# The second q quad of a sliding-window attention made whole and rotated ahead of the attention's rounds

## The chip, the cores and the metric

The kernel runs on one core of one Trainium2 chip. The metric is the device time in microseconds (us); the median of three runs before the change is 1546.49 us (1546.46 to 1546.75). Engines are named as in the profile: PE (matrix products), PEld (its weight loads), DVE and ACT (elementwise work), POOL, and SP, which issues nearly all transfers. Each engine runs its own instructions strictly in the order in which the built program lists them, and waits on semaphores where one needs another engine's result.

## The reference

One layer of a decoder on 1024 tokens of width 1024, all in float32, shortened to what matters here:

```
h = rms_norm(x, ln1_g)
rq, rk, rv, rg, aq, ak, av, gate_a, gate_b = split(h @ w_in + b_in)
branch_a = (silu(rg) * group_norm(retention(rotary(rq), rotary(rk), rv))) @ w_ret_out
aq = rotary(aq.reshape(B, S, 16, 64), pos);  ak = rotary(ak.reshape(B, S, 2, 64), pos)
ay = sliding_window_sink_attention(aq, ak, av, sinks)      # window 128, blocks of 128, softmax with a sink
branch_b = ay @ w_attn_out
x = x + (sigmoid(gate_a) * branch_a + sigmoid(gate_b) * branch_b) @ w_out
x = x + (silu(rms_norm(x) @ w_ffn_gate) * (rms_norm(x) @ w_ffn_up)) @ w_ffn_down
return rms_norm(x, lnf_g)
```

The change lies in the part that makes the attention's q, rotates it, and runs the attention.

## The kernel before, in words

Precision: a float32 operand is split into a high part (a rounding copy on ACT, names with h) and a low part (a subtraction on DVE, names with l). A product is then three PE products per 128-row slice of the contraction: high by high, high by low, low by high (lines 178, 179, 180). One such triple is called a *step*; eight steps fill one 128x512 result bank.

The 16 q heads are made in four *quads* of four heads. A quad (`QuadQ`, `quad_q`) has two halves of the sequence (512 tokens each) and two column groups z (first and second half of each head's elements), so four banks `aq<quad><z><half>` and 32 steps. When a bank is full ACT evicts it with the bias (line 493, `q<quad><z><half>`). When both z of a half are there, `rotation` (lines 508 to 544) makes the rotary of that half: six elementwise products and sums on DVE (line 517, tiles q, st1, st2), two rounding copies on ACT (line 533), two subtractions on DVE (line 536), four stores to a scratch tensor in DRAM and four reads back in the layout the attention needs (lines 524, 529). These pieces are put into a list, `tasks`. For quad 0 the list is emptied at once by `all_tasks`; for the later quads each round of the attention takes one entry.

Beside the quads the list `items` holds eight `Gate`s of 16 steps each (banks `acc_g`). The order is quad 0, quad 1, gate 8, quad 2, gate 9, quad 3, then the other gates. Before an item's products its weights are loaded, rounded (`wh_aq` line 452, `wh_g` line 473, on ACT) and their low part is taken (lines 453, 474, on DVE); this preparation of the next item stands at the 24th step of a quad (or the first or fifth of a gate). The raw weights have two buffers.

The attention runs in 34 *rounds*. Round i works on block i of 32 (quad by quad, eight blocks of 128 tokens each): PE transposes the probabilities of block i-2 (line 619, `pT`), makes the scores of block i (line 584, `s`, one bank pair), DVE and ACT mask them and take the minimum (lines 593 to 596; for the first block of a quad four fused mask-and-minimum instructions at line 599), ACT takes the exponentials of block i-1 (line 607), DVE normalises (610, 611). Then a number of *fill steps* of the items follow on PE, and at the round's end the products with v for block i-2 (line 638, `pv`). Probabilities are split too: rounding copy on ACT (621), low part (622) and masked difference (627) on DVE.

How many fill steps stand in each round is set by three numbers: `early` steps are spread over the first `turn` rounds, `late` over the rest; what is then left of the items runs at the end. Within the rounds a context `in_order` pins PE, SP, ACT, DVE and POOL to the order in which the code emits. What is emitted ahead of it is placed by a list scheduler, which can set it between instructions of the rounds on each engine. In both kernels 28 of the items' 224 steps are left after the rounds.

Of the kernel before, what the change touches and what calls it, by code (L numbers as in the profile page):

```python
# [40 lines left out]
def hybrid_block(ctx: ExitStack, tc: tile.TileContext, x, ln1_g, w_in, b_in, ret_norm_g, w_ret_out,  # L41
# [74 lines left out]
    @contextmanager  # L116
    def in_order(*engines):

        traced = nc.cur_bb.bb.instructions
        last = traced[-1]  # L120
        yield
        start = next(k for k in reversed(range(len(traced))) if traced[k] is last) + 1
        prev = {}
        for i in traced[start:]:
            if i.engine in engines:
                if i.engine in prev:
                    tc.add_manual_dep(i, prev[i.engine],
                                      mybir.DependencyInfo(mybir.DependencyClass.NoSync, mybir.DependencyReason.DATA),
                                      reason="in_order")
                prev[i.engine] = i.name  # L130
# [194 lines left out]
    with tc.tile_pool(name="gt", bufs=1, side="right") as gt, tc.tile_pool(name="w1", bufs=1) as w1:  # L325
# [222 lines left out]
        def task():  # L548
            return tasks.pop(0) if tasks else ([], [], [])

        def do(steps):
            for f in steps:
                f()

        def all_tasks():
            while tasks:
                for part in task():
                    do(part)
            while reads:
                reads.pop(0)()  # L560
# [109 lines left out]
        def filling(n):  # L670
            it = items[n]
            while len(it.w) < it.size:
                prep(it)
            at = 23 if it.size == 2 else 4 if n + 1 < len(items) and items[n + 1].size == 2 else 0
            for k, _ in enumerate(it.products()):
                if k == at and n + 1 < len(items):
                    prep(items[n + 1])
                yield
# [5 lines left out]
        open_s("s_wide")  # L684
        fl = Fill([filling(n) for n in range(1, len(items))])
        NU = 4 * NB
        fl.step(20)
        early, late, turn = 118, 58, 21
        with in_order(nc.tensor.engine, nc.sync.engine, nc.scalar.engine, nc.vector.engine, nc.gpsimd.engine):
            u_sink(0)  # L690
            for i in range(NU + 2):
# [449 lines left out]
    def bb_g(n):  # L1141
        def evac(half, pt):
            c = slice(half * 512, half * 512 + 512)
            t = rt.tile([P, 512], F32, tag="r", bufs=2, name=f"tbr{n}{half}")
            nc.sync.dma_start(t, tb_d[8 + n, :, c])
            m = w2.tile([P, 512], F32, tag="mbw", bufs=1, name=f"mb{n}{half}")
            nc.vector.scalar_tensor_tensor(out=m, in0=t, scalar=1.0, in1=pt, op0=ALU.add, op1=ALU.mult)
            nc.sync.dma_start(mb_d[n, :, c], m)
        return dense_g(w_attn_out, n * P, AY, evac, f"bb{n}")
# [160 lines left out]
    fl = Fill([bb_g(n) for n in range(8)])  # L1310
# [51 lines left out]
    with tc.tile_pool(name="w3", bufs=1) as w3:  # L1362
# [52 lines left out]
        late = in_order(nc.vector.engine, nc.scalar.engine)  # L1415
# [448 lines left out]
    early, kept = [], []  # L1864
# [268 lines left out]
```

## Time and profile before

| | |
|---|---|
| median of three runs | 1546.49 us (1546.46 to 1546.75) |
| the profiled execution's own time | 1546.24 us |
| its span, first to last instruction | 1544.1 us |
| PE busy | 1532.1 us (99%) |
| DVE busy | 1024.5 us (66%) |
| ACT busy | 693.5 us (45%) |
| POOL busy | 386.3 us (25%) |
| mean granted PE clock | 0.999 |
| first scores of the attention (round 0) | start at 78.27 us |
| scores of round 31 | start at 259.28 us |

The span is what the instructions cover; the profiled execution's time is 2.1 us more, which lies outside the instructions. The profile page gives shares over the whole span, so the stretch of the attention (78 to some 265 us) has to be read by windows and by the order in time. A PE product is issued before the one ahead has drained, so its busy time covers small waits: the distance from one start to the next tells more than the idle time.

### The profile page before, as it was taken

How to read it: one execution, taken by the hardware profiler on the slowest of the kernel's cores; microseconds unless marked ns; L12 is line 12 of the kernel's file. 1: busy time of each engine (PE TensorE's matmuls, PEld its weight loads, DVE VectorE, ACT ScalarE, POOL GpSimd, SP SyncE). 2: the span in 40 equal slices, each digit the busy share in tenths (PEclk: the TensorE clock that was granted, in tenths of full speed). 3: DMA queues.
4: the chain of work that ended last, by engine and by line, in shares of the span. 5: the costliest groups of instructions: out<-in, count | busy, mean ns of one | idle time of the engine just before them, and what ended most of it. 6: DMA issues, size and time to landing. Idle time of an engine off the chain costs nothing.

```text
span 1544.1 us, 20386 instructions
## 1 busy us (share of the span) xinstructions
PE 1532.1 (99%) x7299; PEld 1279.8 (83%) x7299; DVE 1024.5 (66%) x1590; ACT 693.5 (45%) x1368; POOL 386.3 (25%) x344
## 2 busy tenths in 40 slices
PE   9999999999999999999999999999999999999998
PEld 8888878888888888888888888888888888888886
DVE  7588897884677764887558688444444444688666
ACT  6366666332344454544223465333333333344445
POOL 2011111002233320000120216555555555100001
PEclk9999999999999999999999999999999999999999
DMA  6656474315766647653657103333333333963332
GB/s 229 187 163 189 144 250 166 103 55 175 207 195 196 213 163 262 206 192 117 204 178 253 68 1 123 109 103 103 102 103 103 103 104 108 318 226 96 92 111 118
DMA packets 158001, 236.85 MB, mean 153 GB/s; under 512 B 10603, under 2 KB 81069, under 8 KB 157645
## 3 DMA queue, kind: packets, MB, share of 16 engines
q1 hardware_dynamic: 155292, 227.04, 45.7%
q0 software_dynamic: 2560, 8.39, 1.5%
q8 instruction: 57, 0.93, 0.3%
q14 instruction: 44, 0.35, 0.1%
q10 hardware_dynamic: 48, 0.13, 0.0%
HBM read 156.62 MB, written 74.19 MB: 149 GB/s over the span
## 4 chain that ended last, share of the span: by engine, by line
PE 94%; DVE 3%; DMA 1%; issue 1%; ACT 1%; SPq 0%; POOL 0%; POOLq 0%; DVEq 0%
PE fA L1757 16%; PE wA L1022 8%; PE fB L1757 8%; PE dA L2059 7%; PE dxP L2059 6%; PE wB L1022 4%; PE fC L1757 4%; PE va L865 3%; PE wo L1591 3%; PE woP L1591 2%; PE wC L1022 2%; PE vP L865 2%; PE aq L178 2%; PE aq L179 2%; PE aq L180 2%; PE acc_ba L180 2%
## 5 line engine op out<-in xcount | busy, mean ns | idle before, releaser
L2059 PE MATMUL dA<-dwP,daP 128*128 128x512 f32 x528 | 120.6, 389 | 0.0
L2059 PEld LDWEIGHTS dA<-dwP,daP 128*128 128x128 f32 x528 | 99.0, 188 | 20.7 <-DVE dwP L154 0.2
L2059 PE MATMUL dxP<-dwP,daP 128*128 128x512 f32 x396 | 90.2, 389 | 0.0
L2059 PEld LDWEIGHTS dxP<-dwP,daP 128*128 128x128 f32 x396 | 74.3, 188 | 15.4
L1832 POOL TENSOR_TENSOR xf<-xf 128x512 f32<-128x512 f32 x40 | 63.9, 1598 | 31.0 <-issue 28.8
L734 POOL TENSOR_TENSOR wr_wp<-wr_wp 128x512 f32<-128x512 f32 x12 | 18.2, 1514 | 193.5 <-DVE w0P L154 92.5
L642 POOL DMA_DIRECT2D xy_d<-xy x32 | 23.1, 723 | 157.2 <-ACT xy L641 98.9
L1763 POOL TENSOR_TENSOR xf<-xf 128x512 f32<-128x512 f32 x33 | 47.3, 1435 | 58.9 <-ACT xf L1765 26.9
L1964 POOL TENSOR_TENSOR rs_f<-tot,mhalf 128x1 f32<-128x1 f32 x8 | 4.9, 607 | 205.4 <-DVE tot L1961 205.4
L154 DVE TENSOR_TENSOR dwP<-wd,dwP 128x512 fp32r<-128x512 f32 x77 | 52.8, 685 | 4.8 <-ACT dwP L151 4.8
L607 ACT ACTIVATE sc<-sc,nm 128x129 f32<-128x129 f32 x128 | 50.1, 402 | 3.6 <-DVE nm L599 3.3
L151 ACT CAST dwP<-wd 128x512 fp32r<-128x512 f32 x77 | 47.4, 616 | 9.1 <-PE dA L2059 6.9
L178 PE MATMUL acc_bb<-ay,wh_bb 128*128 128x512 f32 x128 | 51.0, 400 | 0.0
L151 ACT CAST daP<-daP 128x512 fp32r<-128x512 f32 x42 | 26.0, 621 | 54.8 <-PE dxP L2059 26.7
L180 PE MATMUL acc_bb<-ay,wl_bb 128*128 128x512 f32 x128 | 50.3, 393 | 0.0
L178 PE MATMUL acc_g<-h,wh_g 128*128 128x512 f32 x128 | 50.3, 393 | 0.0
L179 PE MATMUL acc_bb<-ay,wh_bb 128*128 128x512 f32 x128 | 50.2, 392 | 0.0
L178 PE MATMUL aq<-h,wh_aq 128*128 128x512 f32 x128 | 50.2, 392 | 0.0
L179 PE MATMUL aq<-h,wh_aq 128*128 128x512 f32 x128 | 50.0, 391 | 0.0
L179 PE MATMUL acc_g<-h,wh_g 128*128 128x512 f32 x128 | 50.0, 391 | 0.0
L734 POOL TENSOR_TENSOR wr_f<-wr_f 128x512 f32<-128x512 f32 x20 | 30.7, 1533 | 77.2 <-DVE t_6P L154 8.6
L178 PE MATMUL acc_ba<-yg,wh_ba 128*128 128x512 f32 x128 | 49.9, 390 | 0.0
(866 smaller groups left out, 4314.5 us busy)
## 6 DMA issues: line engine op xcount, KB each, us to landing
act_d<-xf SPq DMA_DIRECT2D x77, 256.0 KB, 2.1
daP<-act_d SPq DMA_DIRECT2D x21, 512.0 KB, 3.9
q<-q_d SPq DMA_DIRECT2D x32, 256.0 KB, 4.0
xy_d<-xy POOLq DMA_DIRECT2D x32, 256.0 KB, 3.8
wr_daP<-act_d SPq DMA_DIRECT2D x14, 512.0 KB, 6.7
wr_wp<-in_w_in SPq DMA_DIRECT2D x12, 512.0 KB, 5.4
wp<-in_w_in SPq DMA_DIRECT2D x12, 512.0 KB, 5.2
wd<-in_w_ffn_down SPq DMA_DIRECT2D x6, 1024.0 KB
```

The costliest lines, as they stand in the source:

```text
L151: nc.scalar.copy(hi, raw)
L154: return nc.vector.tensor_tensor(out=lo, in0=raw, in1=f32(hi), op=ALU.subtract)
L178: nc.tensor.matmul(pt, hi[:, k, :], xh, start=(k == 0), stop=False)
L179: nc.tensor.matmul(pt, hi[:, k, :], xl, start=False, stop=False)
L180: nc.tensor.matmul(pt, lo[:, k, :], xh, start=False, stop=(k == 7))
L607: nc.scalar.activation(sc[:, j, 0:P + 1], sc[:, j, 0:P + 1], AF.Exp, scale=-1.0, bias=nm[:, j:j + 1], accum_out=den[:, j:j + 1])
L865: nc.tensor.matmul(vbanks[pr][tt], x_[:, c], w[:, u, :], start=(fresh and k + z == 0), stop=(k == 3 and z == 2), skip_group_check=not fresh)
L1022: nc.tensor.matmul(pt, o[:, w, k, :], v, start=(first and k + z == 0), stop=(k == 3 and z == 2), skip_group_check=not first)
L1591: nc.tensor.matmul(bank, v[:, q + u, k, c], w[y][:, k % 2, :], start=(first and z == 0), stop=(last and z == 2), skip_group_check=not tracked)
L1757: nc.tensor.matmul(pt, o[:, w, k, :], v, start=(first and n == 0), stop=(n == 11), skip_group_check=not first)
L1832: nc.gpsimd.tensor_tensor(out=o, in0=a, in1=b, op=op)
L2059: nc.tensor.matmul(banks[tt], a[:, u, c], w[:, v, :], start=(fresh and f + z == 0), stop=(f == NP - 1 and z == 2), skip_group_check=not fresh)
```

## The change

The number of fill steps ahead of the rounds grows from 20 to 32, which is all of quad 1. Then `all_tasks()` is called, so that both halves of quad 1's rotation are emitted ahead of the rounds instead of as entries of the first rounds. The three numbers become 120 steps over the first 24 rounds (five in each) and 44 over the last ten; they were 118 over 21 and 58 over 13. The sum is the same: 20 + 118 + 58 = 32 + 120 + 44 = 196 steps.

```diff
         open_s("s_wide")
         fl = Fill([filling(n) for n in range(1, len(items))])
         NU = 4 * NB
-        fl.step(20)
-        early, late, turn = 118, 58, 21
+        fl.step(32)
+        all_tasks()
+        early, late, turn = 120, 44, 24
         with in_order(nc.tensor.engine, nc.sync.engine, nc.scalar.engine, nc.vector.engine, nc.gpsimd.engine):
             u_sink(0)
```

What it moves, first on ACT at round 0. Names: `sc00` is the score tile of quad 0, block 0, and the line 607 rows are its four exponentials; `q101` and `q111` are evictions of quad 1's second half; the two line 533 rows with `q100` and `st110` are the rounding copies of the rotation of quad 1's first half; `wh_g8` is the rounding copy of the weights of gate 8, the item after quad 1. Before:

```order
L493 ACTIVATE q110_896<-aq110_871,bcol_91 128x512
L607 ACTIVATE sc00_911,den00_913<-sc00_911,nm00_912 128x129 x4
L493 ACTIVATE q101_951<-aq101_898,bcol_91 128x512
L473 CAST wh_g8_953<-wr_g8_840 128x1024
L593 COPY sc01_935<-s01_968 128x4x128
L621 CAST p00_1010<-pT00_1005 128x512
```

And in the changed kernel:

```order
L493 ACTIVATE q110_896<-aq110_871,bcol_91 128x512
L607 ACTIVATE sc00_998,den00_1000<-sc00_998,nm00_999 128x129
L493 ACTIVATE q101_923<-aq101_898,bcol_91 128x512
L607 ACTIVATE sc00_998,den00_1000<-sc00_998,nm00_999 128x129
L533 ACTIVATE q100_869<-st210_957 128x512
L533 ACTIVATE st110_956<-q110_896 128x512
L607 ACTIVATE sc00_998,den00_1000<-sc00_998,nm00_999 128x129 x2
L473 CAST wh_g8_925<-wr_g8_840 128x1024
L452 CAST wh_aq20_1042<-wr_aq20_842 128x512
```

In both the copy of gate 8's weights stands behind the four exponentials of block 0; in the changed kernel the two rounding copies of quad 1's rotation stand between those exponentials.

On DVE at the same place (line 599: mask and minimum of block 0; line 517: rotation of quad 1's first half; `wl_g8`: low part of gate 8's weights) the order in the changed kernel is:

```order
L536 TENSOR_TENSOR q011_808<-q011_808,st101_810 128x512
L517 TENSOR_TENSOR st210_957<-q100_869,atab_186 128x512
L599 ISA sc00_998,nm00_999<-s00_1002,amask_188,nsink_90 128x128
L599 ISA nm00_999 128x1
L517 TENSOR_TENSOR st110_956<-q110_896,atab_186 128x512
L517 TENSOR_TENSOR q100_869<-q100_869,atab_186 128x512
L517 TENSOR_TENSOR st210_957<-st210_957,st110_956 128x512
L517 TENSOR_TENSOR q110_896<-q110_896,atab_186 128x512
L599 ISA sc00_998,nm00_999<-s00_1002,amask_188,nsink_90 128x128
L599 ISA nm00_999 128x1
L517 TENSOR_TENSOR q110_896<-q110_896,q100_869 128x512
L599 ISA sc00_998,nm00_999<-s00_1002,amask_188,nsink_90 128x128
```

Before, the four line 599 instructions stood together behind the first of these rows, and the rotation of quad 1 came only after `wl_g8`. Now the first line 599 instruction stands ahead of five of the six rotation instructions of quad 1's first half, which are spread among the four.

On PE, the products that follow the first scores before:

```order
L180 MATMUL aq101_898<-h0_118,wl_aq10_778 128x512
L584 MATMUL s00_915<-kst_190,q0_675 128x128 x8
L178 MATMUL aq101_898<-h1_119,wh_aq10_777 128x512
L179 MATMUL aq101_898<-h1_119,wh_aq10_777 128x512
L180 MATMUL aq101_898<-h1_119,wl_aq10_778 128x512
```

and in the changed kernel:

```order
L180 MATMUL aq111_931<-h1_119,wl_aq11_835 128x512
L584 MATMUL s00_1002<-kst_190,q0_675 128x128 x8
L178 MATMUL acc_g8_0_1026<-h0_118,wh_g8_925 128x512
L179 MATMUL acc_g8_0_1026<-h0_118,wh_g8_925 128x512
L180 MATMUL acc_g8_0_1026<-h0_118,wl_g8_926 128x512
```

Before, twelve steps of quad 1 still followed the first scores; now the scores stand behind the whole of quad 1, and the first fill product is gate 8's.

## The prediction

> **What bounds the kernel now.** I read the page first, then the attention's stretch by windows, then the order in time around each place where the change moves something.
>
> ```profile
> PE 1532.1 (99%) x7299; PEld 1279.8 (83%) x7299; DVE 1024.5 (66%) x1590; ACT 693.5 (45%) x1368; POOL 386.3 (25%) x344
> PE 94%; DVE 3%; DMA 1%; issue 1%; ACT 1%; SPq 0%; POOL 0%; POOLq 0%; DVEq 0%
> 200.00:220.00 20.00, 19.50 (x102) 15.93 (x100) 18.74 (x29) 13.87 (x40) 2.81 (x6) 1.00 0.89 284
> 220.00:240.00 20.00, 19.35 (x105) 15.97 (x106) 16.63 (x34) 13.74 (x45) 3.83 (x8) 1.00 0.81 278
> ```
>
> PE is busy 99% of the span and makes 94% of the chain of waits. The change neither adds nor removes a PE product, so it can only alter how long PE waits, and a wait that it adds is never made up later: behind the attention there is no slack on PE. In the windows (PE is the second number) only 200 to 240 us shows PE idle, 0.50 + 0.65 = 1.15 us. That is all there is to gain in idle time; in start distances it is somewhat more:
>
> ```profile
> 212.75 0.62 PE L638 MATMUL pv<-p,vev 128*128 128x512 f32 x2
> 213.21 0.63 PE L638 MATMUL pv<-q,vdf 128*128 128x512 f32 x2
> 213.84 0.63 PE L619 MATMUL pT<-ident,sc 128*128 128x128 f32 x4
> 218.88 0.61 PE L638 MATMUL pv<-p,vev 128*128 128x512 f32 x2
> 220.11 0.73 PE L638 MATMUL pv<-q,vdf 128*128 128x512 f32 x2 [0.62 <-DVE q L627]
> 221.02 0.63 PE L619 MATMUL pT<-ident,sc 128*128 128x128 f32 x4 [0.17 <-DVE sc L611]
> 227.32 1.22 PE L584 MATMUL s<-kst,q 128*128 128x256 f32 x8 [0.37 <-DVE nm L599]
> ```
>
> An undisturbed pair of pv products takes 0.46 us (212.75 to 213.21). At 218.88 the next pair starts 1.23 us later, 0.77 too late; it then takes 0.91 to the transposes, 0.45 too long; the scores at 227.32 lose about 0.5. With the small ones (0.17 at 213.84) some **2.0 us** are lost in rounds 22 to 25, all waiting for a DVE that is full with quad 3's rotation.
>
> **Part 1, twelve steps moved ahead of round 0.**
>
> ```profile
> 78.27 1.00 PE L584 MATMUL s<-kst,q 128*128 128x128 f32 x8
> 79.11 0.45 PE L178 MATMUL aq<-h,wh_aq 128*128 128x512 f32 x1
> 79.87 0.40 PE L178 MATMUL aq<-h,wh_aq 128*128 128x512 f32 x1
> 80.56 0.40 PE L178 MATMUL aq<-h,wh_aq 128*128 128x512 f32 x1
> ```
>
> A step takes 80.56 - 79.87 = 0.69 us, 0.23 a product. Twelve push the first scores back by 8.2 us, to about 86.5, and are missing in the rounds: no cost in the sum.
>
> **Part 2, what follows the first scores.** Before, twelve steps of quad 1 (8.2 us), whose weights were ready, covered the time in which block 0 went through DVE and ACT and gate 8's weights were rounded behind it. Now the first product behind the scores needs those weights at once, so this cover is gone. The chain, each instruction behind the one ahead in its engine's order as listed above:
>
> ```profile
> 79.31 0.35 DVE L599 CUSTOM_DVE_ANT_0 sc<-s,amask,nsink 128x128 f32<-128x128 f32 x1 [6.26 <-PE s L584]
> 79.59 0.35 DVE L599 CUSTOM_DVE_ANT_0 sc<-s,amask,nsink 128x128 f32<-128x128 f32 x1
> 67.70 0.69 DVE L517 TENSOR_TENSOR q<-q,atab 128x512 f32<-128x512 f32 x1
> 68.31 0.69 DVE L517 TENSOR_TENSOR st<-q,atab 128x512 f32<-128x512 f32 x1
> 91.05 0.63 ACT L533 ACTIVATE q<-st 128x512 fp32r<-128x512 f32 x1
> 91.58 0.62 ACT L533 ACTIVATE st<-q 128x512 fp32r<-128x512 f32 x1
> 80.17 0.39 ACT L607 ACTIVATE sc<-sc,nm 128x129 f32<-128x129 f32 x1
> 80.55 0.39 ACT L607 ACTIVATE sc<-sc,nm 128x129 f32<-128x129 f32 x1
> 83.30 1.05 ACT L473 CAST wh_g<-wr_g 128x1024 fp32r<-128x1024 f32 x1 [0.47 <-DMA wr_g<-in_w_in]
> 84.39 1.23 DVE L474 TENSOR_TENSOR wl_g<-wr_g,wh_g 128x1024 fp32r<-128x1024 f32 x1 [2.03 <-ACT wh_g L473]
> ```
>
> Counted from the scores' start: DVE's first mask instruction at 1.04 (79.31 - 78.27), taking 0.28; four rotation instructions at about 0.62 (67.70 to 68.31, a little more where one needs the one before) end at 3.8; the second mask instruction 0.28; the fifth rotation instruction, 0.69 to its end, 4.8. Then ACT's two rounding copies, 0.53 apart, until 5.9: the first writes the tile that this fifth instruction reads, so it can't go earlier. Two exponentials at 0.38: 6.65. The copy of gate 8's weights, 1.05: **7.7**. PE could have gone on at 0.84 (79.11 - 78.27), so it stands **6.9 us**. The raw weights are no bound: in the row at 83.30 they had just landed, ahead of this copy's new start at 86.5 + 6.65 = 93.1. Then the third product of the step needs the low part, 1.23 behind the copy, while two products take 0.46: **0.8 us** more.
>
> Queued behind on DVE: the rest of the rotation; on ACT: the eviction of quad 1's last bank and quad 2's weights; on SP the stores of quad 1, wanted only in round 8. PE alone pays. Bounds: the scheduled order fixes the chain, only the rotation instructions' spacing (0.61 to 0.72) and a semaphore's delay move it, 7.0 to 8.5 for both.
>
> **Part 3, the clock after such a wait.** Two places of the trace show what an idle PE costs afterwards.
>
> ```profile
> 1.02 4.02 PE L290 MATMUL warm<-wk 128*128 128x128 bf16 x36 [1.02 <-DVE wk L261]
> 6.82 0.61 PE L290 MATMUL warm<-wk 128*128 128x128 bf16 x8
> 1533.61 3.33 PE L2059 MATMUL dA<-dwP,daP 128*128 128x512 f32 x14
> 1540.00:1541.00 1.00, 0.00 (x0) 0.00 (x0) 0.00 (x0) 0.17 (x1) 0.00 (x0) 1.00 0.00 0
> 1541.00:1542.00 1.00, 0.00 (x0) 0.00 (x0) 0.00 (x0) 0.00 (x0) 0.00 (x0) 0.54 1.02 422
> ```
>
> At the end PE's last product ends at 1536.94; the granted clock is full until 1541.0 and averages 0.54 in the next us, so it halves about 4.1 us after PE falls idle. At the start 36 products take 4.02 us, some 0.11 each, while the later eight take 0.61 with the last one's drain, some 0.06 each: after an idle stretch the first 4.0 us, at most 5.8 (to 6.82), run at about half speed. An idle of 6.9 us is longer than 4.1, so I expect the clock to halve and cost half of 4.0, 2.0 us. About 0.4 of it is paid in the wait for the low part anyway (two products take 0.86 then). Net **1.6 us**, between 0 and 2.9 - 0.4 = 2.5.
>
> [...]
>
> **Part 4, the rounds.** All 24 first rounds now have five steps, where most had six.
>
> ```profile
> 106.36 1.19 PE L584 MATMUL s<-kst,q 128*128 128x256 f32 x8
> 112.09 1.19 PE L584 MATMUL s<-kst,q 128*128 128x256 f32 x8
> 131.58 0.69 DVE L622 TENSOR_TENSOR p<-pT,p 128x512 fp32r<-128x512 f32 x1 [0.60 <-ACT p L621]
> 135.72 1.22 DVE L474 TENSOR_TENSOR wl_g<-wr_g,wh_g 128x1024 fp32r<-128x1024 f32 x1
> 133.46 0.69 ACT L493 ACTIVATE q<-aq,bcol 128x512 f32<-128x512 f32 x1
> 134.04 1.05 ACT L473 CAST wh_g<-wr_g 128x1024 fp32r<-128x1024 f32 x1
> ```
>
> A five-step round takes PE 5.73 us (106.36 to 112.09). DVE's own part of a round is 4.14 (131.58 to 135.72). Rounds without rotation, which there are more of now, have room. Round 8 has not: gate 9's weights are prepared at quad 2's 24th step, the last of round 7, so DVE stands for the eviction (0.58 to the next start) and the copy (1.05), then does the low part (1.14 of the 1.23), three rotation instructions (1.95), the low part of p (0.7) and its masked difference (1.2): 6.6 us until the pv product can go. PE needs two pairs of pv (0.9), transposes (0.45), scores (0.9), five steps (3.45): 5.7, and one pair more that has what it needs (0.46). So 0.5, and the line 599 block of quad 1 behind it can delay the next scores again by about as much, and the next transposes by 0.3. I take **1.5 us**, bounds 0 (DVE catches up) and 1.8. Round 2 could lose 0.7 to DVE being late from round 0; the half-speed PE gives that time back, so 0.
>
> In rounds 21 to 23 PE has 15 steps instead of 13, 2 x 0.69 = 1.4 us more for a DVE with the same work there. That is taken off the 2.0 us found above: **-1.4 us**, bounds -2.0 and 0.
>
> Sum: 6.9 + 0.8 + 1.6 + 1.5 - 1.4 = **+9.4 us**. The profiled execution took 1546.24, so 1555.6; the median of the runs is 0.25 higher: **1555.8 us**. All low bounds together: 7.0 + 0 + 0 - 2.0 = +5.0; all high: 8.5 + 2.5 + 0.7 + 1.8 = +13.5.
>
> **Rivals.** *The clock stays up.* For: an idle phase of 6.9 us has not been in this trace inside the program. Against: the 4.1 us at its end. Then -1.6, and round 2 costs its 0.7: 1554.9.
>
> *DVE becomes the bound of the shorter rounds.* A quad's six rounds hold 6 x 4.14 + 16 rotation instructions at 0.66 + a gate's low part 1.14 = 36.5 us on DVE against 6 x 5.73 = 34.4 on PE. If the 2.1 us is paid for quad 2 and quad 3 each, instead of the 1.5 in round 8, and the old 2.0 us stays: 7.7 + 1.6 + 4.2 = +13.5, 1560. Against: windows of two or three rounds without rotation lie between, and DVE was at 18.74 of 20 before with little loss.
>
> *No loss: the first fill product doesn't wait.* If gate 8's weights were rounded as soon as they land (83.3 in the row, and the next 1.05 + 1.23 end at 85.6, ahead of PE's need at 87.3), Part 2 and 3 vanish, and what remains is the gain: 1546.24 - 1.4 to -2.0, about 1544.5, no change by measurement. It decides where the copy ends before the first scores do. Against: ACT's list holds the copy behind the exponentials, and an engine that passed a waiting instruction isn't seen in this trace.
>
> **Chances.** Forecast 0.67, clock stays 0.17, DVE bound 0.10, no loss 0.06. A difference within 0.2% (3.1 us) can't be told from no change here; the no-loss case lies there, and only if it also found more than the 2.0 us would it be faster. So slower 0.93, same 0.05, faster 0.02. The range 1551 to 1560.5 takes in the first two cases with their bounds and most of the third.
>
> **What would show it.** After: PE idle of about 7 us ended by ACT wh_g at the product behind the first scores, near 87 to 94 us; a granted clock below 1 in that stretch and products 0.43 apart for some 4 us; a pv wait near round 8; idle in rounds 22 to 25 below 1.15 us. Wrong would be: gate 8's products starting within 1 us of the first scores (Part 2), a clock of 1.00 throughout (Part 3), or idle of more than 2 us in all beyond round 10 (Part 4).

## The result, and the profile after

The changed kernel takes 1556.39 us in the median (1555.36 to 1556.61, six runs) against 1546.64 us for the kernel before (1546.46 to 1546.75, six runs): a ratio of 1.0062, with a 95% interval of 1.0051 to 1.0072. That is 9.8 us slower; the forecast was 1555.8 us. In a later measurement it took 1555.25 against 1546.62 us, 8.6 slower; what may lie behind that difference of 1.1 us is found below.

The profiled execution took 1555.36 us with a span of 1553.6; it is the fastest of the six, 9.1 us above the profiled execution before (9.5 by the spans). First the products of PE in order of time from the first scores on (start, duration, line, tile, idle time before it and its releaser):

```profile
86.35 1.00 PE L584 MATMUL s<-kst,q 128*128 128x128 f32 x8
93.97 0.79 PE L178 MATMUL acc_g<-h,wh_g 128*128 128x512 f32 x1 [6.62 <-ACT wh_g L473]
...
95.83 0.63 PE L178 MATMUL acc_g<-h,wh_g 128*128 128x512 f32 x1
96.25 0.63 PE L179 MATMUL acc_g<-h,wh_g 128*128 128x512 f32 x1
...
98.14 0.40 PE L178 MATMUL acc_g<-h,wh_g 128*128 128x512 f32 x1
98.37 0.40 PE L179 MATMUL acc_g<-h,wh_g 128*128 128x512 f32 x1
...
99.52 1.11 PE L584 MATMUL s<-kst,q 128*128 128x256 f32 x8
```

Gate 8's first product starts 7.62 us behind the first scores; without the wait it would be 0.84, so PE stood 6.78 us. Then products are 0.42 to 0.43 us apart (95.83 to 96.25) until about 97.9, and 0.23 apart afterwards. Round 0, from these scores to the next at 99.52, is 13.17 us long.

The same stretch in the order in time of the two engines that PE waited for, first DVE, then ACT:

```profile
87.39 0.35 DVE L599 CUSTOM_DVE_ANT_0 sc<-s,amask,nsink 128x128 f32<-128x128 f32 x1 [10.08 <-PE s L584]
90.34 0.69 DVE L517 TENSOR_TENSOR q<-q,q 128x512 f32<-128x512 f32 x1
93.95 1.23 DVE L474 TENSOR_TENSOR wl_g<-wr_g,wh_g 128x1024 fp32r<-128x1024 f32 x1
```

```profile
91.07 0.63 ACT L533 ACTIVATE q<-st 128x512 fp32r<-128x512 f32 x1
92.12 0.39 ACT L607 ACTIVATE sc<-sc,nm 128x129 f32<-128x129 f32 x1
92.89 1.03 ACT L473 CAST wh_g<-wr_g 128x1024 fp32r<-128x1024 f32 x1
```

Here the chain of the prediction can be read link by link: the first mask instruction 1.04 us behind the scores, the fifth rotation instruction ending at 91.03, the rounding copies behind it, the last two exponentials, the copy of gate 8's weights from 92.89 to 93.92, PE at 93.97.

By windows of the changed kernel (start and end, length, then the busy time of PE, PEld, DVE, ACT and POOL, the granted PE clock, the DMA share and GB/s):

```profile
94.00:98.00 4.00, 3.96 (x9) 2.72 (x10) 3.93 (x6) 1.03 (x2) 0.00 (x0) 0.52 0.68 206
98.00:102.00 4.00, 4.00 (x23) 3.44 (x22) 3.54 (x6) 2.15 (x4) 0.00 (x0) 1.00 0.48 166
140.00:160.00 20.00, 18.84 (x99) 15.34 (x98) 18.86 (x38) 13.02 (x46) 3.82 (x8) 1.00 0.52 162
...
200.00:220.00 20.00, 20.00 (x109) 17.04 (x109) 17.67 (x28) 13.19 (x40) 2.73 (x6) 1.00 0.87 268
220.00:240.00 20.00, 19.56 (x107) 16.07 (x106) 19.11 (x36) 15.18 (x48) 4.09 (x8) 1.00 0.65 227
```

The granted clock was 0.52 in the 4 us after PE resumed, and full again after 98. From 140 to 160 us PE is idle for 1.16 us, at a place where nothing was idle before; from 200 to 240 the idle time has fallen from 1.15 to 0.44. The new wait near 140 us is round 8, in the order in time of PE in the changed kernel:

```profile
142.62 0.61 PE L638 MATMUL pv<-p,vev 128*128 128x512 f32 x2
143.85 0.73 PE L638 MATMUL pv<-q,vdf 128*128 128x512 f32 x2 [0.61 <-DVE q L627]
144.75 0.63 PE L619 MATMUL pT<-ident,sc 128*128 128x128 f32 x4 [0.17 <-DVE sc L611]
145.75 1.21 PE L584 MATMUL s<-kst,q 128*128 128x256 f32 x8 [0.37 <-DVE nm L599]
...
173.15 0.62 PE L638 MATMUL pv<-q,vdf 128*128 128x512 f32 x2
173.93 0.63 PE L619 MATMUL pT<-ident,sc 128*128 128x128 f32 x4 [0.16 <-DVE sc L611]
...
225.26 0.60 PE L619 MATMUL pT<-ident,sc 128*128 128x128 f32 x4
225.61 1.19 PE L584 MATMUL s<-kst,q 128*128 128x256 f32 x8
```

Against the undisturbed distances (0.46 from one pv pair to the next and from there to the transposes, 0.35 from the transposes to the scores at 225.26) the three steps of round 8 lose 0.77, 0.44 and 0.65: 1.86 us. A second, smaller one is in round 13, 0.32 by these two rows and 0.5 by the length of the round, where DVE makes the low part of quad 3's weights and three rotation instructions in the same round.

### The profile page after: what moved, and what is told of

It is laid out like the page before. It is cut to its first block, busy times and chain, and to the rows that moved or that the text cites. A ratio compares the mean times of both kernels' runs of the same rounds, so it can differ in the third digit from the quotient of the medians.

```text
span 1553.6 us, 20395 instructions
## 1 busy us (share of the span) xinstructions
PE 1534.9 (99%) x7299; PEld 1280.7 (82%) x7299; DVE 1025.3 (66%) x1590; ACT 693.4 (45%) x1368; POOL 390.1 (25%) x344
## 4 chain that ended last, share of the span: by engine, by line
PE 94%; DVE 3%; issue 1%; ACT 1%; DMA 0%; POOL 0%; POOLq 0%; SPq 0%; DVEq 0%
PE fA L1758 15%; PE wA L1023 8%; PE fB L1758 8%; PE dA L2060 7%; PE dxP L2060 6%; PE wB L1023 4%; PE fC L1758 4%; PE va L866 3%; PE wo L1592 3%; PE woP L1592 2%; PE wC L1023 2%; PE vP L866 2%; PE acc_ba L179 2%; PE acc_ba L180 2%; PE acc_ba L178 2%; PE acc_bb L179 2%
## 5 line engine op out<-in xcount | busy, mean ns | idle before, releaser
L180 PE MATMUL acc_g<-h,wl_g 128*128 128x512 f32 x128 | 50.5, 394 | 0.0
```

What stands on the lines that cost most here:

```text
L180: nc.tensor.matmul(pt, lo[:, k, :], xh, start=False, stop=(k == 7))
```

## The experiments

Three questions had to be told apart: which part of the change makes the wait in round 0 and which the rest; what the clock costs, and when it falls; and whether the numbers alone give what the sum took off for the late rounds. Each run is compared with the kernel before on its own chip; differences below are between medians where not said otherwise.

### The steps alone, without the rotation ahead

```diff
         fl.step(32)
-        all_tasks()
         early, late, turn = 120, 44, 24
```

> Edit: the whole of quad 1 ahead of the rounds and the new numbers, but without all_tasks(), so its rotation stays in the rounds. Theory (the first product behind the first scores waits for gate 8's rounded weights, and the rotation set between block 0's exponentials lengthens that chain): the chain without the rotation is some 2.2 us to the last mask result (80.48 - 78.27 in the trace of before), the exponentials, an eviction that stands between them, and the copy of 1.05, so that gate 8's first product comes about 4.6 us behind the scores' start: a wait of 3.8 us, 0.8 more for the low part, 1.4 in round 2, and the 1.8 of round 8 as in the changed kernel. That is shorter than the 4.1 us after which the clock fell at the program's end, so the clock stays full (0.999) and the time is 1553, between 1551.5 and 1554.5. Rival A (the rotation ahead of the attention is the cause, the moved steps cost nothing): 1546 to 1547. Rival B (any wait of this kind costs the clock): 1555, mean clock 0.997 or below. [...]

Measured: 1552.9 us (1552.73 to 1553.6) against 1546.54, ratio 1.0040 (1.0025 to 1.0055).

PE in order of time in this run:

```profile
86.21 1.00 PE L584 MATMUL s<-kst,q 128*128 128x128 f32 x8
90.92 0.79 PE L178 MATMUL acc_g<-h,wh_g 128*128 128x512 f32 x1 [3.70 <-ACT wh_g L473]
```

Gate 8 starts 4.71 us behind the scores, so PE stands 3.87 us (4.71 - 0.84). The rotation between the masks and exponentials therefore makes 7.62 - 4.71 = 2.91 us of the wait, and moving the twelve steps away from behind the first scores makes the other 3.87: ACT's four exponentials and an eviction stand ahead of the copy of the weights even without any rotation. The time was as expected, but by luck: the clock was to stay up after a wait of under 4.1 us, and it fell.

The windows of the same run, columns as above:

```profile
85.50:88.91 3.41, 1.71 (x12) 1.42 (x10) 1.17 (x8) 1.21 (x7) 0.00 (x0) 1.00 0.00 0
88.91:92.32 3.41, 1.36 (x3) 0.64 (x3) 2.29 (x4) 2.48 (x6) 0.00 (x0) 0.50 0.00 0
92.32:95.73 3.41, 3.41 (x8) 2.66 (x9) 0.40 (x1) 0.00 (x0) 0.00 (x0) 0.50 0.55 154
```

These windows are cut so that the clock is constant in each: it fell at 88.91, only 1.7 us after PE had gone idle (at 87.21), and rose at 95.73. On the other side, the loss in round 2 that was expected did not come. Rounds 7 and 8 are together 0.7 us longer than in the changed kernel (5.89 and 8.12 us against 5.73 and 7.56).

### The changed kernel with gate 8's weights rounded ahead of block 0

The first mask instruction and the first exponential of block 0 are put into the ordering chains in which the copies of the weights stand, so that ACT makes the rounding copy and DVE the low part first.

```diff
-                nc.vector.tensor_tensor_reduce(out=sc[:, j, 0:P], ...
+                r = nc.vector.tensor_tensor_reduce(out=sc[:, j, 0:P], ...
+                if u == 0 and j == 0:
+                    tie(vecs, r)
...
-                nc.scalar.activation(sc[:, j, 0:P + 1], ...
+                e = nc.scalar.activation(sc[:, j, 0:P + 1], ...
+                if u == 0 and j == 0:
+                    tie(acts, e)
```

> Edit: the changed kernel, with block 0's first mask instruction on DVE and its first exponential on ACT ordered behind the low part and the rounding copy of gate 8's weights. Nothing else is changed. Theory (wait and clock at round 0 are a matter of that order alone): gate 8's first product follows the first scores within 1 us, the clock is full, and of the 9.75 us of loss 8.3 go; what stays is 0.6 in round 2, 1.8 around round 8, 0.3 in round 13 and 0.8 in rounds 23 to 25, against 2.4 of before: 1548, between 1547 and 1549. Rival (DVE is the bound anyway, the wait only moves to the next scores or to pv): above 1553.

Measured: 1547.72 us (1546.96 to 1548.61) against 1546.54, ratio 1.0007 (0.9997 to 1.0016): no change.

In order of time, first PE, then ACT, of this run:

```profile
86.29 1.00 PE L584 MATMUL s<-kst,q 128*128 128x128 f32 x8
87.13 0.45 PE L178 MATMUL acc_g<-h,wh_g 128*128 128x512 f32 x1
...
90.64 1.11 PE L584 MATMUL s<-kst,q 128*128 128x256 f32 x8
96.56 1.22 PE L584 MATMUL s<-kst,q 128*128 128x256 f32 x8 [0.94 <-DVE sc L594]
```

```profile
85.06 1.05 ACT L473 CAST wh_g<-wr_g 128x1024 fp32r<-128x1024 f32 x1 [2.27 <-DMA wr_g<-in_w_in]
...
87.79 0.41 ACT L609 ACTIVATE sc<-sc,nm 128x129 f32<-128x129 f32 x1
```

(The edit moves the lines behind it; 609 is the old 607.) The copy runs as soon as its weights land, PE goes on 0.84 us behind the scores, and round 0 is 4.35 us long (86.29 to 90.64) instead of 13.17. So 8.8 us of the round hang on the place of this copy and its low part behind block 0 and the rotation, and nearly the whole slowdown goes with it (1556.39 to 1547.72, or 1555.25 to 1547.72). A part of it only moves: round 1 takes 5.92 us (90.64 to 96.56) where the changed kernel has 4.74, as the next scores wait for DVE's masked copy of block 1, which now stands behind the rotation with no wait of PE ahead of it. The rival is right for these 1.2 us and no more. It also answers the rival of no loss: what it needed was exactly this order, and the lists of the changed kernel didn't have it.

### The numbers alone

```diff
         fl.step(20)
-        early, late, turn = 118, 58, 21
+        early, late, turn = 132, 44, 24
```

> Edit: the kernel before, with 20 steps ahead and no all_tasks(), but with 132 steps over the first 24 rounds and 44 over the last ten (20 + 132 + 44 = 196). Theory (the loss of 2.0 us in rounds 22 to 25 of the kernel before comes from too few steps in rounds 21 to 23, and the loss around round 8 from rounds of five steps): rounds of five and six steps stay long enough for DVE, no wait over 0.3 us remains, 1.8 us faster than before: 1544.8, between 1544.3 and 1545.5. Rival (the steps that are missing in the last ten rounds cost there what is won): 1546.6.

Measured: 1545.14 us (1544.3 to 1546.24) against 1546.54, ratio 0.9990 (0.9981 to 0.9999), 1.4 us faster.

Its windows of the late rounds:

```profile
200.00:220.00 20.00, 19.83 (x103) 16.29 (x102) 18.84 (x28) 13.32 (x39) 2.74 (x6) 1.00 0.84 272
220.00:240.00 20.00, 20.00 (x112) 17.05 (x111) 17.10 (x32) 13.79 (x46) 4.25 (x8) 1.00 0.81 282
```

PE is idle for 0.17 us from 200 to 240 instead of 1.15. Against that stands a new wait of 0.8 us in round 1 (scores, for DVE's masked copy), so the waits have been moved as well as taken away, and the expectation that no wait over 0.3 us remains did not hold.

### The rotation alone

```diff
         fl.step(20)
+        all_tasks()
         early, late, turn = 118, 58, 21
```

> The kernel before with one line added: what stands in the list of rotation pieces after the 20 steps is emitted ahead of round 0; steps and numbers stay. My theory says that an early rotation is harmful only through what stands right behind the first scores. Here twelve steps of quad 1 (8.2 us) still stand there, more than the 6.9 us of the chain, so gate 8's weights are ready when PE asks for them: no wait of more than 1.2 us anywhere, clock full, 1546.5 to 1547.8. A rival says that the rotation ahead of round 0 costs its own 2.9 us (the difference of the wait with and without it, 6.9 - 4.0) wherever it is put: 1549.4.

Measured: 1546.46 us (1546.36 to 1547.29) against 1546.49, ratio 1.0001 (0.9992 to 1.0010).

PE in order of time, from round 0 to round 1 of this run:

```profile
82.22 0.39 PE L180 MATMUL aq<-h,wl_aq 128*128 128x512 f32 x1
83.37 1.22 PE L584 MATMUL s<-kst,q 128*128 128x256 f32 x8 [0.77 <-DVE nm L599]
```

The rotation does delay block 0's mask, but all that PE loses there is this one wait of 0.9 us (1.15 from start to start, 0.23 of it the product). The rival's 1549.4 is out: the rotation costs 2.91 us only where no steps with ready weights stand behind the first scores. After 20 steps only the first half of quad 1's rotation is in the list, so this run tests that half alone; it is the half that stands between the exponentials of block 0 in the changed kernel.

### Unread products in the wait

27 further 128x512 products, whose result nobody reads, stand behind the first scores, to keep PE busy in the wait; all else is the changed kernel.

```diff
+                if i == 0:
+                    idle = ps("pv", 1, "idle")
+                    for _ in range(27):
+                        nc.tensor.matmul(idle, H[0][:, 0, 0:P], H[0][:, 0, 0:512], start=True, stop=True)
```

> Edit: the changed kernel with 27 products of 128x512 behind the first scores, into a bank that nothing reads, 27 x 0.23 = 6.1 us of PE work in the wait of 6.9. All else is computed as before. Theory (after the wait the clock costs 1.6 us by itself): the granted clock stays at 0.999, gate 8's products start where they did (94.0 us) and run 0.23 apart; 1.6 us are won, of which round 2 takes back up to 0.7: 1555.2, between 1554.5 and 1555.6, against 1556.4. Rival A (the clock is not what costs; products of gate 8 wait for DVE and ACT anyway): 1556.4. Rival B (the unread products delay gate 8's): above 1556.5.

Measured: 1554.58 us (1554.32 to 1555.28) against 1546.54, ratio 1.0050 (1.0033 to 1.0066). It was run again beside the changed kernel, on one chip:

> The changed kernel itself, as the measure for the two others on the same chip: 1556.4, with runs from 1555.4 to 1557.3 if the clock's fall lasts 6.8 us in some executions and 10.2 in others.

> The 27 unread products behind the first scores again, as the measure for the next: the clock stays full and the executions lie closer together, 1554.4 to 1554.7.

Measured there: the changed kernel 1555.25 us (1554.9 to 1555.91), ratio 1.0054 (1.0041 to 1.0066); with the 27 products 1554.25 (1553.85 to 1554.5), ratio 1.0047 (1.0034 to 1.0059), both against 1546.62. The changed kernel is some 1.1 us below what was expected of it here, the other 0.15 below its range. The rows are of the second run with 27 products:

```profile
86.37 1.00 PE L584 MATMUL s<-kst,q 128*128 128x128 f32 x8
87.21 6.39 PE L710 MATMUL idle<-h 128*128 128x512 f32 x27
94.00 0.50 PE L178 MATMUL acc_g<-h,wh_g 128*128 128x512 f32 x1 [0.40 <-ACT wh_g L473]
...
98.34 1.11 PE L584 MATMUL s<-kst,q 128*128 128x256 f32 x8
...
267.80 1.21 PE L584 MATMUL s<-kst,q 128*128 128x256 f32 x8
```

Gate 8's start hasn't moved (7.63 us behind the scores), the granted clock is 1.00 in the windows of this run from 84 to 98 us (0.999 in the mean of the execution), and round 0 is 11.97 us long. So the wait for the weights and their low part is 11.97 - 4.35 = 7.62 us, and the clock costs the rest: 13.17 - 11.97 = 1.20 us in the changed kernel's first profile. In its profile beside this run round 0 has 12.92 us, so 0.95 there, which agrees with the medians there (1555.25 - 1554.25 = 1.0).

### Half as many unread products

The same with 14 products, which leave PE idle for 3.3 us at the end of the wait.

> The changed kernel with 14 unread 128x512 products (14 x 0.227 = 3.2 us) behind the first scores instead of the 27 of the earlier run: PE then stands for about 3.5 us, from about 90.5 to 94, instead of 6.6. Two rules for the clock: (a) PE must be idle for about 4.1 us, as I had it from the program's end: the clock stays full, 1554.6 as with 27. (b) The clock is set on a grid of 3.41 us and falls after a stretch that is about half idle, as the run with the steps alone suggests (it fell 1.7 us after PE fell idle): an idle time of 3.5 us always fills one such stretch by half, so it falls, and some 3.4 to 6.8 us of products run at half speed: 1556.2 to 1557.5. The start of gate 8's products stays at 93.9 by both.

Measured: 1555.97 us (1555.43 to 1557.52) against 1546.49, ratio 1.0064 (1.0048 to 1.0079).

The windows of this run, again cut where the clock changes:

```profile
87.80:91.21 3.41, 2.78 (x13) 1.93 (x11) 3.41 (x10) 1.76 (x6) 0.00 (x0) 1.00 0.00 0
91.21:94.63 3.42, 0.71 (x2) 0.30 (x2) 3.20 (x9) 3.42 (x9) 0.00 (x0) 1.00 0.63 220
94.63:98.04 3.41, 2.88 (x8) 2.29 (x8) 3.34 (x6) 0.34 (x1) 0.00 (x0) 0.50 0.63 185
```

The clock fell although PE was idle for only 3.34 us (90.58 to 93.92), and it fell at 94.63, when PE had been working again for 0.7 us. That rules out the rule of the prediction, 4.1 us of idle time. From 98.04 on it was full again: the fall lasted one stretch of 3.41 us, the least that was expected, and the median is 0.2 below the expected range; round 0 has 13.30 us, so the clock cost 1.33.

### The late numbers put back

```diff
-        early, late, turn = 120, 44, 24
+        early, late, turn = 106, 58, 21
```

First as a change of the changed kernel:

> The changed kernel, whose 164 steps within the rounds are spread as 106 over the first 21 and 58 over the last 13, so that rounds 21 to 23 have the 13 steps that they had before. My theory says that the five-step rounds there gave back 1.1 to 1.4 us: the waits of rounds 22 to 25 come back in about their old size, 1557.5 to 1557.8. If the late numbers did nothing (the gain was only rotation work that had moved away from there), 1556.4.

Measured: 1556.51 us (1556.3 to 1557.28) against 1546.49, ratio 1.0066 (1.0052 to 1.0079). By the medians alone that looks like the second answer, nothing; against the later measurement of the changed kernel (1555.25) the same median would be 1.3 us higher. The profile says otherwise: from the scores of round 1 to those of round 31 it needs 170.59 us where the changed kernel needs 169.45. What differs as well is the clock, as this run's windows show, cut where it changes:

```profile
86.47:89.88 3.41, 0.54 (x5) 0.39 (x4) 2.84 (x7) 1.07 (x3) 0.00 (x0) 1.00 0.01 2
89.88:93.29 3.41, 0.00 (x0) 0.00 (x0) 3.22 (x11) 3.07 (x9) 0.00 (x0) 0.50 0.29 113
93.29:96.70 3.41, 3.03 (x6) 1.99 (x7) 3.34 (x6) 1.39 (x3) 0.00 (x0) 0.50 0.70 210
96.70:100.12 3.42, 3.42 (x9) 2.64 (x8) 3.05 (x6) 1.05 (x2) 0.00 (x0) 0.50 0.65 215
```

Here it was down for three stretches, 10.2 us, and round 0, whose instructions are the same, took 14.39 us: a cost of 2.42. The clock thus blurred a term of 1.2 us here. So the numbers were compared once more with the clock kept up by the 27 products:

> The 27 unread products and the numbers 106, 58 and 21. In the profiles the numbers alone made the stretch from round 1 to round 31 longer by 1.14 us, but the medians differed by 0.12. If the late term is real and the medians were blurred by the clock, this is 1.1 to 1.3 slower than the 27 products with 120, 44 and 24: 1555.6 to 1555.9. If what the late rounds lose is given back outside them, the two are alike.

Measured: 1555.61 us (1555.11 to 1556.76) against 1546.62, ratio 1.0056 (1.0042 to 1.0070). The mean granted clock was 0.999 in all five executions.

PE in order of time, the scores of rounds 1 and 31 and a product of round 23:

```profile
98.28 1.12 PE L584 MATMUL s<-kst,q 128*128 128x256 f32 x8
...
229.76 0.73 PE L638 MATMUL pv<-q,vdf 128*128 128x512 f32 x2 [0.62 <-DVE q L627]
...
268.93 1.20 PE L584 MATMUL s<-kst,q 128*128 128x256 f32 x8
```

From round 1 to round 31 it takes 170.65 us (98.28 to 268.93) against 169.46 (98.34 to 267.80) with 120, 44 and 24: 1.19 us more. The pv wait of round 23 is back at 229.76. The medians differ by 1.36, but in two of the five executions of this run 2.6 and 3.5 us lay outside the instructions, against 1.7 to 1.8 in the others; the median spans, 1553.4 and 1552.5 us, differ by 0.9, and no span of this run (1553.3 to 1554.1) is as short as the longest with 120, 44 and 24 (1552.1 to 1552.7). The late term is real, at 0.9 to 1.2 us.

### A version that is faster than both

```diff
         fl.step(20)
-        early, late, turn = 118, 58, 21
+        early, late, turn = 136, 40, 24
```

> The kernel before with 20 steps ahead, 136 over the first 24 rounds and 40 over the last ten; no rotation ahead, so nothing of Part 2. It takes four more steps out of the last ten rounds than the run with the numbers alone (132 and 44; 1545.14): if the waits of rounds 22 to 25 are what the numbers win, this can win what was left of the 2.0 us, about 0.5 to 0.8: 1544.3 to 1544.8. If fewer late steps leave DVE the bound in the last rounds, it is slower than 1545.14 by up to 1.

Measured: 1543.86 us (1543.06 to 1544.49, eleven runs) against 1546.49 (21 runs), ratio 0.9982 (0.9973 to 0.9990): 2.6 us faster than the kernel before, and 0.4 below the expected range.

Its windows of the late rounds:

```profile
200.00:220.00 20.00, 20.00 (x108) 17.03 (x107) 18.10 (x28) 13.63 (x46) 4.06 (x8) 1.00 0.81 263
220.00:240.00 20.00, 20.00 (x113) 17.21 (x112) 17.39 (x34) 14.54 (x44) 3.75 (x6) 1.00 0.99 329
```

No idle time of PE is left from 200 to 240 us. What is left is one wait of 1.0 us in round 1, again of the scores for DVE's masked copy. At 0.18% it lies just under what was set as the bound of telling it from no change; its interval, from more runs, leaves out 1.

## Why the prediction was right, point by point

The sum was +9.4 us, the measured difference +9.8 (8.6 in the later measurement). Term by term:

| term | predicted us | measured us | from |
|---|---|---|---|
| wait for gate 8's weights and their low part (Part 2) | 7.7 | 7.62 | round 0 with a full clock, 11.97, less 4.35 |
| clock (Part 3) | 1.6 (0 to 2.5) | 1.20; 0.95, 1.33 and 2.42 in other profiles | round 0 less 11.97 |
| round 8 and other early rounds (Part 4) | 1.5 (0 to 1.8) | 1.86 in round 8, 0.5 in round 13 | order in time |
| late rounds (Part 4) | -1.4 (-2.0 to 0) | -1.19 (profiles), -0.9 (median spans) | 27 products with either set of numbers |

**Part 2** held link by link: it was read from the order of DVE's and ACT's lists with durations from the kernel before. Putting the copy and its low part first took it out of round 0 whole, and 1.2 us came back in round 1 (the second experiment). The split into steps (3.87) and rotation (2.91) shows that either half of the edit alone behaves differently: the rotation alone (its first half) costs 0.9 us in its profile and nothing that the medians show, the steps alone cost 6.4 us.

**Part 3** had a cost of about the right size, from a rule that is wrong; that the size came out is in part luck. That the clock "halves about 4.1 us after PE falls idle" was read from one place, the program's end, and made into a threshold. It fell 1.7 us after PE went idle in the steps alone, and after an idle time of 3.34 us with 14 products. What the profiles show in its place: the changes of the clock lie whole multiples of 3.41 us apart (one with 14 products, two with the steps alone, three with the late numbers put back; 25, 2 and 425 in the changed kernel), and it fell at the end of a stretch of that length in which PE was busy for 1.71 us (the steps alone), 0.71 (14 products) or 0.54 (the late numbers), and in the changed kernel (87.57 to 90.99) not at all, while a stretch with 2.78 (87.80 to 91.21, 14 products) left it up. The end of the kernel before fits the same grid: from 1534.25 to 1537.67 PE was still busy for 2.70 us, from there to 1541.08 not at all, and then the clock fell; the 4.1 us were the distance from the last product to that point. How much was then paid differed from profile to profile, and so did the place of these stretches: one began 1.22 us behind the first scores in the changed kernel and 0.47 with the late numbers put back, and the same wait for gate 8's weights (7.62 and 7.63 us from the scores) cost 1.20 us in the one and 2.42 in the other. In the changed kernel's second profile it cost 0.95. What sets the place of the stretches, no run shows.

That their place is also why the changed kernel's medians are 1.1 us apart in the two measurements is only argued: of the timed executions only the span and the mean clock are on record. The mean is 0.995 to 0.996 in the first measurement and 0.996 to 0.997 in the second, which points that way. But the fall at the program's end moves this mean as well: in the first profile, with a mean of 0.996, the clock is low for 6.83 us in round 0 and for 5.12 us at the end.

**Round 2** was to lose 0.7 us if the clock stayed up, because DVE would be late from round 0. With a full clock it lost nothing: rounds 1 and 2 are as long with the 27 products as without, 4.74 and 5.27 us. It was close: in that run DVE's masked copy of block 1 ends at 102.82, 0.26 us ahead of round 2's scores. Where the wait of round 0 was taken away, the same scores lost 1.2 us (the second experiment).

**Part 4** had the right place, engine and instructions for round 8, and the three waits that it named came: pv 0.77, transposes 0.44 and scores 0.65, where 0.5, 0.3 and "about as much" as 0.5 were worked out. What was too small is the list of such rounds: the prediction said that rounds without rotation "have room", priced round 8, and put nothing for any other round that has rotation. Round 13, where quad 3's weights are prepared, lost 0.5. The same kind of stretch, a weight preparation and rotation in one five-step round, was there to be found. Together the early rounds cost 2.4 instead of 1.5. The late term was right within 0.2 by the profiles, within 0.5 by the spans.

The measured terms add up to 7.62 + 1.20 + 2.36 - 1.19 = 10.0. The scores of round 31 stand 9.69 us later than before (268.97 to 259.28); the 0.3 between them is mostly round 1, which is 0.2 us shorter against its number of steps than it was. The spans differ by 9.5, the medians by 9.8, so that the account closes to about half a us. The errors are -0.4 us in Part 3, +0.9 in the early and +0.2 in the late rounds: they cancelled only in part.

**The rivals.** The clock didn't stay up, so that one is out, though its time (1554.9) lies within 0.4 us of the later measurement. DVE as the bound of all five-step rounds is out: from round 3 to round 23 all but rounds 8, 13 and 23 take 5.71 to 5.76 us, which is PE's own time for five steps, or 5.27 where one pv pair fewer is due (rounds 10 and 18). No loss at the first fill product is out by the row at 93.97, and became true when the copy was put first.

## What to carry to other kernels

Work that is moved ahead of a stage takes with it what covered the stage's start: look for the first product behind the new boundary, and follow its operands back through the lists of the other engines, since a copy that is ready to run waits behind everything listed ahead of it (gate 8's until 92.89 us; put first, it ran at 85.06). A threshold for the clock that is read from one place is not a rule: here one and the same wait cost 0.95, 1.20 and 2.42 us in three profiles, so cost such a wait from its least to its most. When an effect of 1 us is to be measured beside such a wait, keep PE busy in it first; the medians here hid a term of about 1 us, and showed it once the clock stayed up.

## What was not expected of the hardware

The changes of the granted clock lay whole steps of 3.41 us apart: in the changed kernel it was full from 5.66 to 90.99 us (25 such steps), low until 97.82 (two), and full from there until 1548.48 (425). It fell after a half-busy stretch (1.71 us of 3.41 in the steps alone, at 88.91), and even while PE was already at work again (with 14 products at 94.63, PE having started at 93.92).

The ends of two programs say more about how busy a stretch was that left the clock up. There the last 128x512 products run out at a different place of the grid. The two windows, first of the run with 14 unread products, then of the changed kernel:

```profile
1545.29:1548.70 3.41, 1.55 (x7) 0.94 (x5) 2.56 (x6) 1.83 (x5) 0.55 (x1) 1.00 0.54 223
1545.07:1548.48 3.41, 1.39 (x7) 0.81 (x5) 2.38 (x6) 1.66 (x5) 0.67 (x2) 1.00 0.58 237
```

After the first the clock stayed full for one more stretch, to 1552.12, which the mean clock on record for this execution, 0.998, agrees with (a fall at 1548.70 would make it 0.997); after the second it fell at once, at 1548.48. So at these two ends 1.55 us of 3.41 left it up and 1.39 did not. The stretch at 85.50 in the steps alone had 1.71 and fell all the same; 1.00 us of it is the eight 128x128 products of the scores, so the busy time of the profile is not the whole measure. What else counts stays open.

How busy a stretch was that raised it stays open too: 2.88 us of 3.41 raised it with 14 products (94.63 to 98.04), and 3.03 did not with the late numbers put back (93.29 to 96.70); PE's busy time is modelled at the ends of products, so that these two may not be as close as they look.
